# Branch A's channel pairs by seven block products, placed ahead of q, k, v, with z and gates behind

## The chip, the core and the metric

The kernel runs on one core of a Trainium2 chip. A core has TensorE (matrix products out of SBUF into the eight banks of PSUM), VectorE, ScalarE and GpSimd (elementwise work), SyncE, and DMA queues that SyncE, ScalarE and GpSimd issue to. The metric is device time in microseconds from the first to the last work of one execution; less is better.

## The reference

One decoder layer with two parallel branches, over a prompt of 1024 tokens and a sample of 8 sequences of 4 tokens (1056 tokens in all, 1024 channels, 8 heads of 128). All is float32.

```python
u = rmsnorm(x, norm_w)
a_b, a_c, a_h, a_z, qkv, b_z, b_beta, b_alpha, g_a, g_b = split(u @ w_in)
conv_out, new_a_buf = causal_conv(a_c * a_h, conv_a_buf, conv_a_w)      # width 3
y_a = (silu(a_z) * a_b * conv_out) @ w_out_a
q, k, v = silu(causal_conv(qkv, conv_qkv_buf, conv_b_w))                # width 4
o, S_new = gated_delta(l2norm(q) * 128**-0.5, l2norm(k), v, beta, g, S0)
y_b = (rmsnorm_head(o) * silu(b_z)) @ w_out_b
y = rmsnorm(x + (sigmoid(g_a) * y_a + sigmoid(g_b) * y_b) @ w_o, final_norm_w)
```

Within a chunk of tokens the gated delta rule needs the inverse of a unit lower triangular matrix and the products with decays; from chunk to chunk a state per head is carried on. The states of the convolutions and of the delta rule are outputs too.

## The kernel before

Tokens lie along the free axis, channels on the partitions. The normed input is kept in SBUF as two parts, uh (rounded) and ul (the rest), and every weight block of 128 output channels likewise as wh and wl; `mm` (L194) adds wh*uh, wl*uh and wh*ul over eight channel groups. A block is taken in three slices of 352 tokens (BLK, NBLK), 24 matmuls each, into one of four PSUM banks `pp`; other products use four banks `pd`. `load_w` fetches a block on SyncE's queue and splits it on ScalarE (L147) and VectorE (L149) while the block before it is in use; a list `seq` gives the order.

The order: x is loaded, normed, transposed (L270) and split; beta, alpha and the first k run in between; then the decay matrices `ee` of all heads are built from a DRAM scratch `gscr` (`gb`, L384 to L386); then for each head k, q and v (blocks, convolution, chunk products, results to DRAM scratch); then z (8 blocks, `act_proj`), branch A (for each of 8 channel groups the blocks c, h, z, b), the gates g_b and g_a (8 blocks each). Then follow w_out_a (8 blocks) on Y_A's factor, which `ya_` keeps in SBUF, w_out_b (8 blocks), and w_o (L928).

Behind the blocks from z on runs background work, written as generators: `invert` (the inverse, all on VectorE, L525 and L528, 62 steps), `merge` (of its halves, 18 steps, last product L567), `sample` (the delta rule of the sample, 27 steps), `scan` (the prompt's chunks, eight times two groups of four heads, 80 steps; loads `ld`, `tt`, `sz` on GpSimd's queue from L720). `pump` takes `rate` steps after each slice of a block; the rate is 1.1 up to the sample and 1.85 for the scan. Each generator's SBUF pool takes the place of the one before it, and `drain` runs the rest. During w_out_a the scan's result `oscr` is loaded and split for w_out_b (`o32`, one buffer, L883, L866, L867).

All of this is put into an order by a planner that simulates the engines and lets an instruction that is ready go ahead of others on its engine; `keep_in_program_order` pins one behind what was written before it on that engine.

Of the kernel before, what the change touches and what calls it, by code (L numbers as in the profile page):

```python
# [16 lines left out]
P = 128  # L17
D = 1024
# [7 lines left out]
NBLK = 3  # L26
NH = 8
# [20 lines left out]
def hybrid_step(ctx, tc, x_prompt, x_sample, state_conv_a, state_conv_qkv, state_delta, w_in, conv_a_w,  # L48
# [13 lines left out]
    pp = ctx.enter_context(tc.tile_pool(name="pp", bufs=4, space=PSUM))  # L62
    pd = ctx.enter_context(tc.tile_pool(name="pd", bufs=4, space=PSUM))
    dram = ctx.enter_context(tc.tile_pool(name="dram", bufs=1, space=DRAM))
    wp = ctx.enter_context(tc.tile_pool(name="wp", bufs=2))
    yp = ctx.enter_context(tc.tile_pool(name="yp", bufs=1))

    def ytile(k, shape=(P, TT)):
        return yp.tile(list(shape), F32, tag=f"ya{k}", name=f"ya{k}")

    def ptile(n=512):
        return pp.tile([P, n], F32, tag="pp", name="pp")

    def dtile(n=512):
        return pd.tile([P, n], F32, tag="pd", name="pd")
# [8 lines left out]
    oscr = dram.tile([NH, P, TT], F32, name="oscr")  # L84

# [1 line left out]
    ident = const.tile([P, P], F32, name="ident")  # L87
    make_identity(nc, ident)
    s_m, mid = opened(name="mid", bufs=1)
# [21 lines left out]
    newa = mid.tile([P, 18, 8], F32, name="newa")  # L111
    beta = mid.tile([P, 9, NH], F32, name="beta")
# [10 lines left out]
    s_m2, mid2 = opened(name="mid2", bufs=1, side="right")  # L123
    pastq = mid2.tile([P, 24, 24], F32, name="pastq")
    pasta = mid2.tile([P, 8, 16], F32, name="pasta")
    newq = mid2.tile([P, 27, 24], F32, name="newq")
    smp = mid2.tile([P, 3, NH, TS], F32, name="smp")
    szs = mid2.tile([P, NH, TS], F32, name="szs")
    gsb = mid2.tile([P, 2, 64, NT], F32, name="gsb")
    egs = mid2.tile([P, 64, NT], F32, name="egs")  # L130
    eps_ = mid2.tile([P, 6, 64], F32, name="epairs")

# [4 lines left out]
    s_u, up = opened(name="up", bufs=1)  # L137
# [4 lines left out]
    def load_w(w, col):  # L142
        n = 16 if w is w_in and col == C_BA else P
        wr = wp.tile([P, KC, n], F32, name="wr")
        nc.sync.dma_start(wr, w[:, col:col + n].rearrange("(k p) c -> p k c", p=P))
        wh = wp.tile([P, KC, n], F32R, name="wh")
        act.copy(wh, wr)  # L147
        wl = wp.tile([P, KC, n], F32R, name="wl")
        dve.tensor_tensor(wl, wr, wh.bitcast(F32), op=ALU.subtract)  # L149
        return wh, wl  # L150

    # every weight block is fetched and split while the one before it is in use
    seq = [(w_in, C_BA)]
    for h in range(NH):
        seq += [(w_in, C_K + h * P), (w_in, C_Q + h * P), (w_in, C_V + h * P)]
    seq += [(w_in, C_BZ + h * P) for h in range(NH)]
    for c in range(KC):
        seq += [(w_in, base + c * P) for base in (C_AC, C_AH, C_AZ, C_AB)]
    seq += [(w_in, base + c * P) for base in (C_GB, C_GA) for c in range(KC)]
    seq += [(w, c * P) for w in (w_out_a, w_out_b) for c in range(KC)]  # L160
    loaded = []
# [20 lines left out]
    def begin(w, col, mh, ml, ahead=True):  # L182
        assert seq[0][0] is w and seq[0][1] == col
        seq.pop(0)
        if not loaded:
            loaded.append(load_w(w, col))
        wh, wl = loaded.pop(0)
        if seq and ahead:
            loaded.append(load_w(*seq[0]))
# [31 lines left out]
    def conv_begin(ci):  # L221
# [3 lines left out]
        def evac(b, ps):  # L225
# [3 lines left out]
            if b == NBLK - 1:  # L229
                act.copy(sv[:, :, 3:7], ps[:, n:n + TS].rearrange("p (b t) -> p b t", t=NT))  # L230
# [741 lines left out]
```

## Time and profile before

| | us |
|---|---|
| median of 3 runs | 1473.81 |
| lowest, highest run | 1473.34, 1474.85 |
| profiled execution, span | 1474.3 |
| TensorE busy in it | 1430.8 (97%) |
| VectorE, ScalarE, GpSimd busy | 718.6, 459.9, 373.4 |

The profiled execution's own time is its span; it lies 0.5 us over the median of the runs. Matmuls are pipelined and a matmul's duration overlaps that of the next, so the distance between the starts of two matmuls is what one costs. The granted clock is given as a share of TensorE's full 2.4 GHz; the level below it is 1.2 GHz.

### The profile page before, as it was taken

The page shows a single profiled execution, that of the slowest core. Times are in us where ns is not written, and L with a number is a line of the kernel's source. Part 1 is how long each engine was busy: PE and PEld are TensorE (multiplying, and loading weights), DVE is VectorE, ACT ScalarE, POOL GpSimd, SP SyncE. Part 2 cuts the span into 40 slices and gives each one's busy share as a digit, 9 for nine tenths or more (in the row PEclk, how much of TensorE's full clock was granted, in tenths as well). Part 3 has the DMA queues.
Part 4 walks back from the last instruction along what each step waited for, and adds up shares of the span by engine and source line. Part 5 has one row for each costly group of instructions (what it writes and reads, how often), then busy time and mean ns, then how long its engine had stood idle before and what let it go on. Part 6 is the DMA issues. An engine that isn't in the chain of part 4 may idle for free.

```text
span 1474.3 us, 22239 instructions
## 1 busy us (share of the span) xinstructions
PE 1430.8 (97%) x9045; PEld 1373.8 (93%) x9045; DVE 718.6 (49%) x1262; ACT 459.9 (31%) x1120; POOL 373.4 (25%) x544
## 2 busy tenths in 40 slices
PE   8995899999999999999999999999999999999997
PEld 6995899999999999999999989999999999999785
DVE  6545454554548899994342543222222263355422
ACT  6436465555522111111110101333323331123111
POOL 2135543333240011113422244222221120001100
PEclk9997999999999999999999999999999999999999
DMA  5265675554383211115334166555765344343411
GB/s 171 63 100 101 157 199 130 131 141 114 97 229 104 73 43 44 44 44 143 95 91 131 32 179 208 180 180 182 244 224 183 117 148 131 100 145 111 152 43 47
DMA packets 135594, 186.18 MB, mean 126 GB/s; under 512 B 7735, under 2 KB 106177, under 8 KB 133444
## 3 DMA queue, kind: packets, MB, share of 16 engines
q0 software_dynamic: 26976, 108.10, 26.5%
q1 hardware_dynamic: 104480, 63.25, 14.7%
q10 hardware_dynamic: 4036, 13.41, 2.4%
q8 instruction: 71, 1.16, 0.3%
q14 instruction: 31, 0.25, 0.1%
HBM read 128.56 MB, written 56.18 MB: 125 GB/s over the span
## 4 chain that ended last, share of the span: by engine, by line
PE 85%; DMA 6%; issue 3%; POOL 2%; DVE 2%; ACT 1%; SPq 0%; DVEq 0%; POOLq 0%; ACTq 0%
PE pp L194 68%; PE pp L928 6%; DMA gb<-gscr 1%; PE pd L464 1%; DMA sb<-in_state_delta_dram 1%; PE pd L761 1%; PE pd L746 1%; PE pd L740 1%; DMA scr<-pk 1%; PE pd L729 1%; PE pd L760 1%; PE pd L622 1%; PE pd L683 1%; DMA qd<-gscr 1%; PE pd L567 1%
## 5 line engine op out<-in xcount | busy, mean ns | idle before, releaser
L194 PE MATMUL pp<-uh,wh 128*128 128x352 f32 (+1 forms) x1944 | 641.5, 330 | 0.0
L194 PE MATMUL pp<-uh,wl 128*128 128x352 f32 (+1 forms) x1944 | 632.1, 325 | 6.1 <-DVE wl L149 6.1
L194 PE MATMUL pp<-ul,wh 128*128 128x352 f32 (+1 forms) x1944 | 634.0, 326 | 0.0
L194 PEld LDWEIGHTS pp<-uh,wl 128*128 128x128 f32 (+1 forms) x1944 | 366.5, 189 | 11.1 <-DVE wl L149 6.7
L194 PEld LDWEIGHTS pp<-uh,wh 128*128 128x128 f32 (+1 forms) x1944 | 365.8, 188 | 5.6 <-issue 2.2
L194 PEld LDWEIGHTS pp<-ul,wh 128*128 128x128 f32 (+1 forms) x1944 | 365.5, 188 | 3.8 <-issue 2.0
L149 DVE TENSOR_TENSOR wl<-wr,wh 128x1024 fp32r<-128x1024 f32 (+1 forms) x97 | 130.7, 1347 | 183.5 <-ACT wh L147 183.2
L147 ACT CAST wh<-wr 128x1024 fp32r<-128x1024 f32 (+1 forms) x97 | 101.4, 1045 | 226.9 <-PE pp L194 225.7
L400 DVE SCALAR_TENSOR_TENSOR cv<-ext,vecT,cv 128x1080 f32<-128x1080 f32 x72 | 100.0, 1389 | 3.5 <-ACT cv L398 1.9
L701 ACT ACTIVATE zt<-pp 128x352 f32<-128x352 f32 x72 | 33.4, 465 | 180.9 <-PE pp L194 180.2
L525 DVE TENSOR_TENSOR pr<-xi,dl 128x1 f32<-128x1 f32 (+36 forms) x156 | 84.6, 542 | 5.1 <-POOL xi L511 0.8
L528 DVE TENSOR_REDUCE xi<-pr 128x1 f32<-128x1 f32 (+36 forms) x156 | 83.7, 537 | 4.8 <-DVE pr L525 0.2
L194 PE MATMUL pp<-yh,wh 128*128 128x352 f32 x192 | 62.2, 324 | 1.5 <-ACT yh L866 1.5
L194 PE MATMUL pp<-oh,wl 128*128 128x352 f32 x192 | 62.4, 325 | 0.0
L194 PE MATMUL pp<-yh,wl 128*128 128x352 f32 x192 | 62.2, 325 | 0.0
L194 PE MATMUL pp<-oh,wh 128*128 128x352 f32 x192 | 62.0, 323 | 0.0
L194 PE MATMUL pp<-ol,wh 128*128 128x352 f32 x192 | 61.8, 322 | 0.0
L194 PE MATMUL pp<-yl,wh 128*128 128x352 f32 x192 | 60.4, 325 | 1.4 <-POOL yl L867 1.3
L928 PE MATMUL pp<-woh,mh 128*128 128x512 f32 (+1 forms) x144 | 57.2, 397 | 1.1 <-ACT woh L911 1.1
L928 PE MATMUL pp<-wol,mh 128*128 128x512 f32 (+1 forms) x144 | 56.4, 395 | 0.0
L928 PE MATMUL pp<-woh,ml 128*128 128x512 f32 (+1 forms) x144 | 56.3, 391 | 0.0
L464 PE MATMUL pd<-kq 128*128 128x256 f32 x128 | 35.5, 403 | 16.6 <-ACT pk L442 16.6
(296 smaller groups left out, 1838.4 us busy)
## 6 DMA issues: line engine op xcount, KB each, us to landing
wr<-in_w_in_dram SPq DMA_DIRECT2D x80, 512.0 KB, 4.0
ld<-scr POOLq DMA_DIRECT2D x16, 1280.0 KB, 6.9
scr<-pk POOLq DMA_DIRECT2D x16, 768.0 KB, 4.4
sb<-in_state_delta_dram POOLq DMA_DIRECT2D x16, 512.0 KB, 4.9
zscr<-zt ACTq DMA_DIRECT2D x8, 528.0 KB, 2.6
gbscr<-zt ACTq DMA_DIRECT2D x8, 528.0 KB, 4.1
gascr<-zt ACTq DMA_DIRECT2D x8, 528.0 KB, 3.3
sg<-gascr POOLq DMA_DIRECT2D x8, 528.0 KB, 4.2
```

Of the source, the lines that this page charges most:

```text
L147: act.copy(wh, wr)
L149: dve.tensor_tensor(wl, wr, wh.bitcast(F32), op=ALU.subtract)
L194: pe.matmul(ps[:a.shape[2], :BLK], lhsT=a[:, k, :], rhs=m[k][:, sl], start=(k == 0 and i == 0), stop=(k == KC - 1 and i == 2))
L400: dve.scalar_tensor_tensor(cv, ext[:, j:j + LB], vecT[:, j * 24 + ci:j * 24 + ci + 1], cv, op0=ALU.mult, op1=ALU.add)
L464: pe.matmul(pt[:, i * 256:(i + 1) * 256], lhsT=kq[:, 0, c * P:(c + 1) * P], rhs=kq[:, :, c * P:(c + 1) * P], start=True, stop=True)
L525: ins = dve.tensor_tensor(pv, xi[q][:, 0:n, c0:j], bc(dl[j // Q4][:, j % Q4, c0:j], 1, [P, n, w]), op=ALU.mult)
L528: dve.tensor_reduce(xi[q][:, 0:n, j], pv, axis=AX.X, op=ALU.add, negate=True)
L567: pe.matmul(px[:64, h * H2:(h + 1) * H2], lhsT=t11[:, h, :], rhs=ww[:, h, :], start=True, stop=True)
L622: pe.matmul(pks[:, n * 8:(n + 1) * 8], lhsT=sb[:, b, :], rhs=kqn[:, :, n * NT:(n + 1) * NT], start=True, stop=True)
L683: pe.matmul(pt, lhsT=ktw[:, 0, g, :], rhs=we[:, hf * 4:(hf + 1) * 4, :].rearrange("p b v -> p (b v)"), start=True, stop=True)
L701: ins = act.activation(t[:, b * BLK:(b + 1) * BLK], ps[:, :BLK], func)
L928: pe.matmul(ps[:n, :], lhsT=a[k][:, sl], rhs=w[k][:, cs_], start=(k == 0 and i == 0), stop=(k == KC - 1 and i == 2))
```

## The change

Branch A goes in front of q, k, v. Its first channel group is done as before. For the other seven, the blocks c and h make a pair, and z and b another: 14 pairs. A pair is a 2 by 2 block product (two blocks of output channels, two halves of the tokens; the two halves of the input channels are summed over). It is done with seven products of four channel groups by 528 tokens, each in two slices of 264 (QT) and with the three matmuls of the split, in place of eight such products. The weight sums are made on VectorE ahead of each product (`prep`), the token sums once (`token_sums`, four calls, 12 VectorE instructions each); the seven results are combined in PSUM, by ScalarE copies (`kept`) and in the evictions. PSUM is laid out for it as three double banks `pb`, taken in turn, and two banks `pd`; x's transposes use both. After branch A the four and four banks of before are set up.

z, g_b and g_a follow q, k, v as 24 plain blocks. The background is one generator `chain` of the four parts at rate 2.0, and goes on through w_out_a. Y_A's factor goes to DRAM (`yscr`) and is loaded and split ahead of w_out_a; w_out_a's result goes to DRAM (`ascr`) too. After `drain` the scan's result is loaded through one buffer and split, and `ascr` is loaded, for w_out_b. The decay matrices are built two heads at a time between the heads. The norm's weight is broadcast by DMA and no longer by four matmuls.

```diff
+HT = TT // 2
+QT = HT // 2
...
     def ptile(n=512):
-        return pp.tile([P, n], F32, tag="pp", name="pp")
+        if "pb" in pools:
+            return btile()[:, 0, :n]
+        return pools["pp"].tile([P, n], F32, tag="pp", name="pp")
+    def btile():
+        i = nb[0] % 3
+        nb[0] += 1
+        return pools["pb"].tile([P, 2, 512], F32, tag=f"pb{i}", name=f"pb{i}")
...
+    PRODS = (1, 5, 6, 3, 7, 2, 4)
+    def prep(u):
...
+        if p == 5:
+            sums[pid] = sw.tile([P, 4, P], F32, tag="s", name="s1", bufs=2)
+            dve.tensor_tensor(sums[pid], a21, a22, op=ALU.add)
+        elif p == 6:
+            dve.tensor_tensor(sums[pid], sums[pid], a11, op=ALU.subtract)
+        elif p == 3:
+            dve.tensor_tensor(sums[pid], a12, sums[pid], op=ALU.subtract)
+        elif p == 7:
+            s3 = sw.tile([P, 4, P], F32, tag="s", name="s3", bufs=2)
+            dve.tensor_tensor(s3, a11, a21, op=ALU.subtract)
+        src = {1: a11, 2: a12, 4: a22, 7: s3 if p == 7 else None}.get(p, sums.get(pid))
+        w2 = wp.tile([P, 2, 4, P], F32R, tag="hl", name="w2", bufs=4)
+        act.copy(w2[:, 0], src)
+        dve.tensor_tensor(w2[:, 1], src, w2[:, 0].bitcast(F32), op=ALU.subtract)
+        return w2
...
+    def project_pair(c0, c1, evac):
...
+        def product(p, ps, start):
+            w2 = take()
+            th, tl = tok[p]
+            for g in range(2):
+                sl = slice(g * QT, (g + 1) * QT)
+                for k in range(4):
+                    for i, (a, m) in enumerate(((w2[:, 0], th), (w2[:, 1], th), (w2[:, 0], tl))):
+                        pe.matmul(ps[:, g, :QT], lhsT=a[:, k, :], rhs=m[:, k, sl], start=start and k == 0 and i == 0,
+                                  stop=(k == 3 and i == 2), skip_group_check=True)
+            return ps[:, :, :QT]
...
+        x, z = btile(), btile()
+        p1 = kept(product(1, x, True), "p1", 1)
+        p5 = kept(product(5, z, True), "p5", 2)
+        u2 = kept(product(6, x, False), "u2", 1)
+        evac(0, 1, product(3, z, False), u2)
+        evac(1, 1, product(7, x, False), p5)
+        evac(0, 0, product(2, btile(), True), p1)
+        evac(1, 0, product(4, x, False), None)
...
+    def token_sums(k):
...
+        r11, r12 = whole(tmp("p1", "r11"), 0, 0), whole(tmp("u2", "r12"), 0, HT)
+        r22, t3 = whole(tmp("p5", "r22", 2), 1, HT), tmp("s", "t3", 2)
+        dve.tensor_tensor(t3, r22, r12, op=ALU.subtract)
+        split(7, t3)
...
-        for i in range(2):
-            pt = ptile()
-            pe.matmul(pt, lhsT=ones[0:1, :], rhs=nwr[:, i * 512:(i + 1) * 512], start=True, stop=True)
-            dve.tensor_copy(nwb[:, i * 512:(i + 1) * 512], pt)
+    nc.scalar.dma_start(nwb, norm_w[0].partition_broadcast(P))
...
-            pt = dtile()
+            pt = dtile() if half else ptile()
...
+    token_sums(0)
+    for ci in range(KC):
+        branch_a(ci)
+        if ci == 1:
+            decays()
...
+        conv_chunk(8 + h, kq[:, 0])
         if h == 0:
-            conv_end(8, kq[:, 0], ext_k0, sv_k0)
+            decay_matrices(0)
+            decay_matrices(1)
+        elif h % 2 and h < NH - 1:
+            decay_matrices(h + 1)
+            decay_matrices(h + 2)
...
+    def chain():
+        for nm, fn, bufs in (("fp", invert, 1), ("fq", merge, 1), ("sp", sample, 1), ("cp", scan, 2)):
+            held, pl = opened(name=nm, bufs=bufs, side="right")
+            yield from fn(pl)
+            held.close()
+
+    background.append(chain())
+    rate[0] = 2.0
+    for h in range(NH):
+        act_proj(C_BZ + h * P, AF.Silu, zscr, h, szs[:, h, :])
     for h in range(KC):
-        act_proj(C_GB + h * P, AF.Sigmoid, gbscr, h, first=(h == 0))
+        act_proj(C_GB + h * P, AF.Sigmoid, gbscr, h)
     for h in range(KC):
         act_proj(C_GA + h * P, AF.Sigmoid, gascr, h, kouter=h == KC - 1)
...
+    for k in range(KC):
+        y32 = op_.tile([P, TT], F32, name="y32")
+        nc.sync.dma_start(y32, yscr[k])
+        pairs_.append(split(ha, y32, "y"))
...
+        nc.sync.dma_start(ascr[e], m)
+    drain()
...
+    for e in range(KC):
+        o32 = op_.tile([P, TT], F32, name="o32")
         aux.dma_start(o32, oscr[e])
         opair.append(split(hb, o32, "o"))
+    for e in range(KC):
+        ma.append(ytile(e))
+        nc.sync.dma_start(ma[e], ascr[e])
```

## Rows read from the trace of the kernel before

**Rows 1.** The page's first two parts: busy time per engine; granted clock in 40 slices.

```profile
PE 1430.8 (97%) x9045; PEld 1373.8 (93%) x9045; DVE 718.6 (49%) x1262; ACT 459.9 (31%) x1120; POOL 373.4 (25%) x544
...
PEclk9997999999999999999999999999999999999999
```

**Rows 2.** The page's chain that ended last, shares by engine.

```profile
PE 85%; DMA 6%; issue 3%; POOL 2%; DVE 2%; ACT 1%; SPq 0%; DVEq 0%; POOLq 0%; ACTq 0%
```

**Rows 3.** Busy time by stretch: length, engines with instructions, PEclk, DMA share, GB/s.

```profile
0.00:36.00 36.00, 28.98 (x162) 22.08 (x163) 24.55 (x40) 22.84 (x43) 9.12 (x26) 1.00 0.57 175
...
75.00:196.00 121.00, 98.04 (x570) 94.58 (x568) 57.71 (x70) 62.68 (x169) 61.79 (x74) 0.90 0.66 130
196.00:400.00 204.00, 204.00 (x1288) 200.86 (x1287) 102.89 (x153) 115.25 (x371) 70.91 (x133) 1.00 0.50 132
400.00:664.00 264.00, 264.00 (x1662) 263.59 (x1662) 215.50 (x376) 51.06 (x83) 42.14 (x64) 1.00 0.28 82
664.00:746.00 82.00, 82.00 (x696) 78.72 (x696) 31.66 (x41) 13.97 (x21) 31.90 (x45) 1.00 0.42 115
746.00:898.00 152.00, 149.91 (x895) 139.32 (x894) 71.03 (x190) 20.21 (x28) 51.31 (x49) 0.98 0.43 116
898.00:1182.00 284.00, 282.49 (x1968) 281.26 (x1966) 75.63 (x173) 96.50 (x283) 68.79 (x90) 1.00 0.57 191
1182.00:1273.00 91.00, 89.57 (x552) 88.84 (x552) 37.24 (x42) 18.57 (x19) 11.71 (x17) 1.00 0.41 124
```

**Rows 4.** Pieces of the chain of waits: start us, us, what.

```profile
415.91 276.07 PE pp L194 x1736
...
1379.98 86.94 PE pp L928 x372
```

**Rows 5.** Timeline of TensorE at three places: start us, us, instructions merged.

```profile
23.13 0.32 PE L194 MATMUL pp<-uh,wh 128*16 128x352 f32 x1
23.29 0.32 PE L194 MATMUL pp<-uh,wl 128*16 128x352 f32 x1
...
777.94 1.85 PE L622 MATMUL pd<-kqn,sb 128*128 128x8 f32 x16
...
1021.34 1.05 PE L740 MATMUL pd<-r,tt 128*128 128x128 f32 x8
```

**Rows 6.** Groups by line and shape: count, busy us, mean ns, idle before.

```profile
L149 DVE TENSOR_TENSOR wl<-wr,wh 128x1024 fp32r<-128x1024 f32 x96 | 130.4, 1358 | 183.5 <-ACT wh L147 183.2
...
L275 DVE TENSOR_TENSOR ul<-pd,uh 128x512 fp32r<-128x512 f32 x16 | 10.3, 681 | 1.0 <-ACT uh L274 1.0
...
L866 ACT CAST oh<-o 128x1056 fp32r<-128x1056 f32 x8 | 8.6, 1075 | 27.3 <-DMA o<-oscr 27.3
...
L867 DVE TENSOR_TENSOR ol<-o,oh 128x1056 fp32r<-128x1056 f32 x8 | 10.1, 1256 | 18.3 <-ACT oh L866 18.3
...
L525 DVE TENSOR_TENSOR pr<-xi,dl 128x1 f32<-128x1 f32 (+36 forms) x156 | 84.6, 542 | 5.1 <-POOL xi L511 0.8
L528 DVE TENSOR_REDUCE xi<-pr 128x1 f32<-128x1 f32 (+36 forms) x156 | 83.7, 537 | 4.8 <-DVE pr L525 0.2
```

**Rows 7.** Single lines: duration ns min/median/max, first and last start us.

```profile
L528 DVE TENSOR_REDUCE xi<-pr x156: 148/513/1204, 422.3 to 671.1; 128x1 f32<-128x1 f32 x4, 128x2 f32<-128x4 f32 x4, 128x3 f32<-128x9 f32 x4, 128x4 f32<-128x16 f32 x4
...
L567 PE MATMUL pd<-ww,t x128: 217/218/267, 697.6 to 745.5; 64*64 64x64 f32 x128
...
L701 ACT ACTIVATE zt<-pp x72: 455/464/480, 403.6 to 1174.9; 128x352 f32<-128x352 f32 x72
...
L720 POOL DMA_DIRECT2D ld<-scr x16: 534/536/597, 899.0 to 1123.2; - x16
```

**Rows 8.** DMA issues: count, KB each, median us from issue to landing.

```profile
ld<-scr POOLq DMA_DIRECT2D x16, 1280.0 KB, 6.9
...
gb<-gscr POOLq DMA_DIRECT2D x8, 512.0 KB, 8.9
...
o<-oscr POOLq DMA_DIRECT2D x8, 528.0 KB, 3.9
```

More of the change, by code (lines that the diff above doesn't have):

```diff
@@ L153, in hybrid_step @@
-    seq = [(w_in, C_BA)]
-    for h in range(NH):
[L155 to L161, printed above, removed]
+    tok = {}
+    PRODS = (1, 5, 6, 3, 7, 2, 4)
@@ new lines, in hybrid_step, with plan, plan_pair, w_cols @@
+    units, pairs, ready, raw, sums = [], [], {}, {}, {}
+    pos, nraw = [0], [0]
+    def plan(w, col):
+        units.append(("c", w, col))
+    def plan_pair(w, c0, c1):
+        pairs.append((w, c0, c1))
+        units.extend(("s", len(pairs) - 1, p) for p in PRODS)
+    def w_cols(w, col, n):
+        return w[:, col:col + n].rearrange("(k p) c -> p k c", p=P)
+    def fetch(pid, x):
+        if pid >= len(pairs):
+            return
+        i = nraw[0] % 3
+        nraw[0] += 1
+        t = pools["sw"].tile([P, KC, P], F32, tag="wx", name="wx") if i == 2 else wp.tile([P, KC, P], F32, tag="wr",
+                                                                                         name="wr")
+        nc.sync.dma_start(t, w_cols(pairs[pid][0], pairs[pid][1 + x], P))
+        raw[pid, x] = t
@@ new lines, in take @@
+    def take(ahead=True):
+        i = pos[0]
+        pos[0] += 1
+        if units[i][0] == "s":
+            at = PRODS.index(units[i][2])
+            if at in (0, 4):
+                fetch(units[i][1] + 1, at // 4)
+        room = 4
+        for j in range(i, min(i + 3 if ahead else i + 1, len(units))):
+            room -= 1 if units[j][0] == "s" else 0 if units[j][2] == C_BA else 2
+            if room < 0:
+                break
+            if j not in ready:
+                ready[j] = prep(units[j])
+        return ready.pop(i)
@@ new lines, in hybrid_step @@
+    plan(w_in, C_BA)
+    for base in (C_AC, C_AH, C_AZ, C_AB):
+        plan(w_in, base)
+    for c in range(1, KC):
+        plan_pair(w_in, C_AC + c * P, C_AH + c * P)
+        plan_pair(w_in, C_AZ + c * P, C_AB + c * P)
+    for h in range(NH):
+        for base in (C_K, C_Q, C_V):
+            plan(w_in, base + h * P)
+    for base in (C_BZ, C_GB, C_GA):
+        for h in range(NH):
+            plan(w_in, base + h * P)
+    for w in (w_out_a, w_out_b):
+        for c in range(KC):
+            plan(w, c * P)
@@ L182, in begin @@
     def begin(w, col, mh, ml, ahead=True):
[L183 to L189, printed above, removed]
+        u = units[pos[0]]
+        assert u[0] == "c" and u[1] is w and u[2] == col
+        wh, wl = take(ahead)
         def mm(ps, b, k):
@@ L707, in act_proj, with scan_step @@
         act.dma_start(dst[h], t)
-    background.append(invert())
-    rate[0] = 1.1
-    for h in range(NH):
-        act_proj(C_BZ + h * P, AF.Silu, zscr, h, szs[:, h, :])
     GH = 4
     state = [None, None]
-    def scan_step(c, g):
+    def scan_step(cp, c, g):
         hs = slice(g * GH, (g + 1) * GH)
@@ L780, in scan_step, with scan @@
         yield
-    def scan():
+    def scan(cp):
         for c in range(NCH):
-            gens = [scan_step(c, g) for g in range(2)]
+            gens = [scan_step(cp, c, g) for g in range(2)]
             while gens:
```

499 lines of the change are left out of this document (288 added, 211 removed).

## The prediction

> **What bounds the kernel now.** I read the page first. TensorE is busy for 97% of the span and its granted clock is full in all but a few slices [rows 1]; the chain that ended last is 85% TensorE [rows 2]. So whatever is to help must take work off TensorE, and whatever is to hurt must make TensorE wait. The table by stretches [rows 3] then shows where it waits today: 23 us out of 75 to 196 us (98.04 busy of 121, at a mean clock of 0.90), where the first heads wait for decay matrices, and hardly anywhere else. In the long stretch 400 to 1273 us the idle time is 2.1 + 1.5 + 1.4 = 5 us.
>
> Next the price of one matmul. 1736 of them, 352 columns wide, took 276.07 us: 159.0 ns each; 372 with 512 columns took 86.94 us: 233.7 ns [rows 4]. One block of 128 output channels is 72 matmuls, 11.45 us. Is that price the columns' or the weight load's? A 16-column stationary block has the same spacing, 23.13 to 23.29 us, so it is the columns. And 16 matmuls of 8 columns with full 128x128 weights fit into 1.85 us [rows 5], about 0.115 us each: that is the weight load's floor, and it lies under the column price of anything wider than 260.
>
> Last the background work (inverse, merge, sample, scan). It is one serial chain, today fed in behind 56 blocks and ended before the output projections. Its pieces [rows 7] tell how long it is when it isn't held back, which is what the change will ask.
>
> **Branch A's pairs.** Each of 14 pairs replaces 2 x 72 = 144 matmuls of 352 columns by 7 x 24 = 168 of 264. 264 columns were never run here. In proportion to 352 they take 159.0 x 264/352 = 119.3 ns; on the line through 352 and 512 columns 117.9; if the 12.3 ns that 352 columns take above 352/2.4 stay whole, 122.3. I take 119.3, since both widths measured are 8 to 10% above the columns at 2.4 GHz. A pair falls from 22.90 to 20.04 us, 14 pairs save **40.0 us** (33 to 43). VectorE must keep up: 7 subtractions and 4 sums over 512 columns at 0.68 [rows 6] are 7.5 us, five evictions over 528 columns some 3.5, so 11 of 20 us, 14 where the convolution's two passes fall in. That is hidden; uncovered it would be the saving and more.
>
> The Trainium skill, "TensorE: Matmul & The Clock Gate", section on the back-to-back issue gap, puts a warm matmul at N/2.4 plus about 2.5 ns. That would be 149.2 and 112.5 ns, and 36.2 us saved. The 352-column row disagrees, 159.0, so the measured price goes into the sum.
>
> **The first 90 us.** Before, matmuls of the first two blocks run between the transposes of x: in the first 36 us there are 162 matmuls [rows 3], of which 72 are transposes and 4 the norm's broadcast, so 86 are projection work, 13.7 us of it. After the change half of the transposes and the projections draw on the same three PSUM buffers in turn, so the first projection must wait until the seventh x block is evicted. I lose **8 us** (0 to 13.7). Then 48 VectorE passes for the token sums, 0.70 each, 33.6 us, plus 14 us of splits, evictions, convolution and first weight sums, stand against three blocks, 34.4 us of TensorE. The overhang is 14 us if nothing is done earlier; the planner moves ready work ahead, as the interleaved transposes show, so I take **5 us** (0 to 14). The norm weight's broadcast by DMA in place of four matmuls I set at nothing: x is fetched at the same time.
>
> **The start of q, k, v.** Today eight broadcasts of decays, 8.9 us each [rows 8], stand in front of the first heads, with VectorE and ScalarE queued behind them. Moved two at a time between heads, with the scratch written some 250 us earlier, they are out of the way; the per-head broadcast of the other decay stays and so does the first head's latency. **-22 us** (-10 to -32). The later heads run without gaps (204.00 of 204) and stay as they are.
>
> **The chain behind z and gates.** Here the change costs. Branch A's 32 blocks leave the stretch in which the chain ran. The first z eviction begins at 403.6 [rows 7], so z begins at 399.8; the last output projections begin at 1273. Between them lie 873.2 us: 64 blocks (732.8), 5 idle, so some 135 us of the chain's own TensorE work. After the change TensorE has 32 blocks there, 366.4, and the same 135: 501 us. Does the chain fit into 501?
>
> Step by step, from the beginning of z. The inverse starts at 422 [rows 7]: 22 us, of which most are its loads. Its 312 VectorE instructions take 84.6 + 83.7 = 168.3 us [rows 6], about 12 more between them, and a weight split of 1.36 falls in with every block, 17 of them, 23: 203 us. It can't be hastened by feeding it faster; at rate 2 it is VectorE that paces it, and the splits overtake it as they do now (in 400 to 664 VectorE is busy for 215.50 us and TensorE never waits). From its end, 671.6, to the merge's last matmul at 745.5 and copy, 746.6: 75 us of stores, loads and eight serial steps. The sample goes on to 898: 151 us, paced by sixteen loads of half a megabyte. The scan's first load is issued at 899.0 and takes 6.9 [rows 7, 8]: 10. One chunk of the scan, unhindered: the load of the next waits for the last product of this one, 6.9, then three groups of eight matmuls at 1.05 [rows 5], two rounds of VectorE and ScalarE of about 1, and the output product of sixteen matmuls, 1.8, with handovers 15; two groups share TensorE and DMA, so 17. Eight chunks: 136. The last output, its norm and store: 8. Sum 606. I take **580**, because the rows of merge and sample stood in a stream full of blocks, and the blocks run out at about 415 us, within the sample. Ends: 510 (merge and sample a fifth shorter, scan at 14 a chunk) and 650 (scan at 22). The chain is longer than the 501 us of TensorE work by 79, and TensorE waits for it.
>
> **The loads of branch B's output.** Today eight loads of 528 KB, each split before the next can use the buffer, are hidden behind w_out_a. One round is 3.9 to land [rows 8], 1.07 and 1.26 for the split [rows 6], 6.4 with handovers: 51 us. Now they stand behind the end of the chain, with nothing to cover them but the first product as far as PSUM holds it, some 13 us. **+38 us** (20 to 55; the loads of branch A's result run beside them). The reloads of Y_A's factor ahead of w_out_a cost nothing as long as the chain is what is late; without it they cost some 10.
>
> **Sum**, against the profiled span of 1474.3: in front of z, +366.4 (32 blocks) - 40.0 + 8 + 5 - 22 = +317.4. From z to the last projections, 580 + 38 - 873.2 = -255.2. Together +62.2, a span of 1536.5. The median of the runs lies 0.5 us under the profiled span, so **1536 us**.
>
> **The rivals.** *The chain fits behind the blocks* (faster). For it speaks that 187 steps at two a group end before the 192 that the blocks give out, so the order written down ends in time; against it that a step can't be run before its data are there. With TensorE as the bound, 501 us and 10 of reloads: 511 + 38 - 873.2 + 317.4 = -6.8, 1467 us; with the loads hidden too 1430. It decides from a chain under 518 us. *The emptied TensorE falls to its lower clock.* In 75 to 196 us, with 81% busy, the mean granted clock was 0.90; in a scan alone it is busy for about 60%. Every product of the scan then takes twice as long, some 5.5 us a chunk on its chain: +44, 1580 us. The Trainium skill, the same page's part on the clock gate's oscillation, says likewise that gaps between bursts bring the array back to half rate; the row agrees. *The narrower matmuls are not cheaper in time*: at 136.3 ns a piece, from weight loads (0.19 us each) or VectorE, the 40 us are gone: 1576 us. Against it stand rows 5.
>
> **Chances.** My forecast 0.58, with its own range 1500 to 1565 (chain 550 to 610); the chain that fits 0.16, of which 0.03 come out level; the lower clock 0.18; no cheaper matmuls 0.08. A difference of 0.2%, 3 us, is about what can be told from none. Faster 0.13, same 0.03, slower 0.84. The range takes in the lower clock and the edge of the chain that fits: 1465 to 1595.
>
> **What would show it.** Right: the 264-column matmuls 119 ns apart; z begins near 717; the inverse fills VectorE for some 200 us; TensorE has gaps from some 420 us after z's beginning until the last projections, with the scan alone on it; then eight split rounds of about 6.4 us with little TensorE work. Wrong: w_out_a's matmuls still running when the scan ends, then the chain was shorter than its rows; or TensorE waiting in branch A for weight sums.

## The result and the profile after

The changed kernel takes 1607.93 us (median of 4 runs, 1605.23 to 1609.61) against 1474.33 for the kernel before beside it: a ratio of 1.0905 [1.0883, 1.0926]. Slower, as forecast, but by 134 us instead of 62, and outside the range that ended at 1595. The profiled execution has a span of 1607.9 us, against 1474.3 before, and the sum of the prediction was 1536.5: **71.4 us are to be explained.**

The page first: busy time per engine, then TensorE's granted clock in 40 slices. They answer to [rows 1].

```profile
PE 1458.3 (91%) x9377; PEld 1381.1 (86%) x9377; DVE 837.6 (52%) x1464; ACT 520.3 (32%) x1224; POOL 373.9 (23%) x549
...
PEclk8999999999899999999999999899857777589999
```

TensorE fell from 97% of the span to 91%, and a dip has appeared between slices 30 and 36. The chain that ended last, 85% TensorE before [rows 2], follows only some 13% of the span here, so the stages are read from single lines instead: duration of one in ns (min/median/max), first and last start.

```profile
L304 PE MATMUL pb<-uh,w x672: 278/283/294, 93.0 to 377.6; 128*128 128x264 f32 x168
L955 ACT ACTIVATE zt<-pp x72: 447/464/577, 725.7 to 1002.8; 128x352 f32<-128x352 f32 x72
L785 DVE TENSOR_REDUCE xi<-pr x156: 143/506/1206, 752.2 to 984.0; 128x1 f32<-128x1 f32 x4, 128x2 f32<-128x4 f32 x4, 128x3 f32<-128x9 f32 x4, 128x4 f32<-128x16 f32 x4
L966 POOL DMA_DIRECT2D ld<-scr x16: 534/537/597, 1192.1 to 1335.3; - x16
L1099 POOL DMA_DIRECT2D o<-oscr x8: 528/528/556, 1363.3 to 1414.6; - x8
```

In order: the 2352 matmuls of the pairs fill 93.0 to 380.9, 121.9 ns apart. The first z eviction is at 725.7, so z begins at 721.9, where the sum has 399.8 + 317.4 = 717.2. The inverse starts at 752.2, 30 us after z, and ends at 984.3. The scan's first load is issued at 1192.1, its last store of output at 1362.6, and at 1363.3 the loads of branch B's output begin. From z's beginning to there are 641.4 us; the forecast for this chain was 580. Behind it come 244.6 us, where 201 + 38 = 239 were forecast. So 4.7 + 61.4 + 5.6 = 71.7, the 71.4 but for rounding: **by these marks nearly the whole error is the chain.** The mark for z's beginning turns out to be some 9 us off in the kernel before; the part on why the prediction was off says what that moves.

Where TensorE has nothing to do in it shows in the stretches from the inverse to the first product with `w_out_b` (the columns of [rows 3]):

```profile
752.00:985.00 233.00, 233.00 (x1467) 232.94 (x1466) 192.27 (x338) 48.54 (x82) 13.60 (x21) 1.00 0.37 107
985.00:1053.00 68.00, 64.09 (x556) 60.57 (x555) 24.38 (x29) 18.27 (x24) 25.02 (x37) 0.92 0.83 217
1053.00:1192.00 139.00, 119.05 (x633) 101.61 (x631) 60.27 (x184) 7.35 (x7) 43.52 (x42) 0.84 0.57 167
1192.00:1363.00 171.00, 115.34 (x672) 102.33 (x672) 47.50 (x146) 50.04 (x208) 59.67 (x83) 0.73 0.60 208
1363.00:1423.00 60.00, 29.79 (x95) 26.95 (x96) 10.34 (x9) 9.61 (x9) 5.13 (x10) 0.56 0.42 140
```

The third column is TensorE's. In the inverse it is full; in merge, sample, scan and the loads behind them it lacks 4 + 20 + 56 + 30 = 110 us, where before it lacked 5 in the whole of 664 to 1273 [rows 3]. What it waits for, over the whole span (total us, times, longest):

```profile
PE pp L266 <- ACT oh L1065: 32.9, 8, 9.6
PE pd L1020 <- ACT on L1016: 26.8, 16, 2.6
PE pd L986 <- DMA tt<-tscr: 17.6, 2, 15.2
...
PE pd L940 <- POOL we L934: 13.0, 5, 3.2
PE pd L605 <- DMA pq<-in_state_conv_qkv_dram: 12.3, 1, 12.3
```

The first four lines are the split of branch B's output, the scan and the sample. The last was not foreseen. The history of q, k, v moved with its stage to the end of branch A. Two of its three loads are issued at once, at 378.8 and 381.1. The third stands on ScalarE's queue behind exponentials of the decay matrices, which wait for their broadcasts; it is issued at 407.65, and TensorE waits 12.3 us for it.

And the inverse on VectorE, 752 to 985 (group, busy us, mean ns, idle just before it and what ended that):

```profile
L782 DVE TENSOR_TENSOR pr<-xi,dl 128x1 f32<-128x1 f32 (+36 forms) x156 | 84.7, 543 | 5.3 <-POOL xi L770 0.2
L785 DVE TENSOR_REDUCE xi<-pr 128x1 f32<-128x1 f32 (+36 forms) x156 | 83.8, 537 | 4.8
L185 DVE TENSOR_TENSOR wl<-wr,wh 128x1024 fp32r<-128x1024 f32 x20 | 24.5, 1226 | 21.8 <-ACT wh L183 21.8
L751 DVE COPY so<-pd 120x128 f32<-120x128 f32 (+2 forms) x6 | 1.7, 285 | 8.3 <-DMA out_dram<-so 8.3
```

The inverse's own work is what the prediction took from [rows 6], 168.5 us. But the third line shows VectorE idle for 21.8 us in front of the weight splits: the split stands at the head of VectorE's queue, waits for ScalarE's rounding, which waits for a buffer of weights, and the inverse's next step, ready to run, stands behind it. The fourth line stands for stores of states through one small buffer. They were there before; now branch A's state is stored with them, and VectorE waits 8.3 us for the buffer within the inverse's stretch. In the kernel before, over its inverse (422 to 672), these two waits are 16.9 and 3.3 us:

```profile
L149 DVE TENSOR_TENSOR wl<-wr,wh 128x1024 fp32r<-128x1024 f32 x22 | 32.4, 1475 | 16.9 <-ACT wh L147 16.9
L492 DVE COPY so<-pd 120x128 f32<-120x128 f32 (+1 forms) x4 | 1.1, 283 | 3.3 <-DMA out_dram<-so 3.3
```

### The profile page after: what moved, and what is told of

Same layout as the page of the kernel before. It is cut to its first block, busy times and chain, and to the rows that moved or that the text cites. A ratio compares the mean times of both kernels' runs of the same rounds, so it can differ in the third digit from the quotient of the medians.

```text
span 1607.9 us, 23413 instructions
## 1 busy us (share of the span) xinstructions
PE 1458.3 (91%) x9377; PEld 1381.1 (86%) x9377; DVE 837.6 (52%) x1464; ACT 520.3 (32%) x1224; POOL 373.9 (23%) x549
## 5 line engine op out<-in xcount | busy, mean ns | idle before, releaser
L266 PE MATMUL pp<-uh,wh 128*128 128x352 f32 x1152 | 374.8, 325 | 0.0
L266 PE MATMUL pp<-ul,wh 128*128 128x352 f32 x1152 | 373.9, 325 | 0.0
L266 PE MATMUL pp<-uh,wl 128*128 128x352 f32 x1152 | 370.6, 322 | 0.0
L266 PEld LDWEIGHTS pp<-uh,wh 128*128 128x128 f32 x1152 | 216.7, 188 | 2.2 <-ACT ext L644 1.5
L266 PEld LDWEIGHTS pp<-uh,wl 128*128 128x128 f32 x1152 | 217.1, 188 | 0.4
L266 PEld LDWEIGHTS pp<-ul,wh 128*128 128x128 f32 x1152 | 216.8, 188 | 0.5
L304 PE MATMUL pb<-uh,w 128*128 128x264 f32 x672 | 124.0, 284 | 0.0
L304 PEld LDWEIGHTS pb<-uh,w 128*128 128x128 f32 x672 | 103.9, 188 | 0.0
L658 DVE SCALAR_TENSOR_TENSOR cv<-ext,vecT,cv 128x1080 f32<-128x1080 f32 x72 | 96.8, 1344 | 12.3 <-ACT cv L656 10.6
L304 PE MATMUL pb<-ul,w 128*128 128x264 f32 x336 | 95.2, 283 | 0.0
L782 DVE TENSOR_TENSOR pr<-xi,dl 128x1 f32<-128x1 f32 (+36 forms) x156 | 84.7, 543 | 5.3 <-POOL xi L770 0.2
L785 DVE TENSOR_REDUCE xi<-pr 128x1 f32<-128x1 f32 (+36 forms) x156 | 83.8, 537 | 4.8
L304 PEld LDWEIGHTS pb<-ul,w 128*128 128x128 f32 x336 | 63.3, 188 | 0.0
```

Of the source, the lines that this page charges most:

```text
L266: pe.matmul(ps[:a.shape[2], :BLK], lhsT=a[:, k, :], rhs=m[k][:, sl], start=(k == 0 and i == 0), stop=(k == KC - 1 and i == 2))
L304: pe.matmul(ps[:, g, :QT], lhsT=a[:, k, :], rhs=m[:, k, sl], start=start and k == 0 and i == 0, stop=(k == 3 and i == 2), skip_group_check ...
L658: dve.scalar_tensor_tensor(cv, ext[:, j:j + LB], vecT[:, j * 24 + ci:j * 24 + ci + 1], cv, op0=ALU.mult, op1=ALU.add)
L782: ins = dve.tensor_tensor(pv, xi[q][:, 0:n, c0:j], bc(dl[j // Q4][:, j % Q4, c0:j], 1, [P, n, w]), op=ALU.mult)
L785: dve.tensor_reduce(xi[q][:, 0:n, j], pv, axis=AX.X, op=ALU.add, negate=True)
```

## The experiments

Each is an edit of the changed kernel unless it says otherwise. The changed kernel's stages (z begins 721.9, inverse 752.2 to 984.3, scan 1192.1 to 1363.3) are the comparison.

**1. The pairs taken out, the order kept.**

```diff
-        plan_pair(w_in, C_AC + c * P, C_AH + c * P)
-        plan_pair(w_in, C_AZ + c * P, C_AB + c * P)
+        for base in (C_AC, C_AH, C_AZ, C_AB):
+            plan(w_in, base + c * P)
...
```

> The changed order kept, the 14 pairs done as plain blocks, no token sums. The chain theory (the time from the beginning of z to the last step of the scan is set by the serial chain, everything in front by TensorE): the front grows by 14 x (144 x 159.0 - 168 x 121.9 ns) = 34 us less the token sums' 0 to 5 us, so about 1608 + 31 = 1639 us (1632 to 1645), the chain unchanged at some 641 us. Rival, the pairs themselves cost the time (VectorE sums, narrower matmuls): 1608 us or less.

1630.96 us (1629.72 to 1635.15), ratio 1.105 [1.102, 1.108]. The first z eviction comes at 745.4, 19.7 later, and the chain behind it is the same, 643.9. The stretch of the pairs itself is 32.7 longer; 12.3 of the difference is given back at the wait for `pq`, which only the faster branch A runs into. So the pairs are a real gain, worth some 23 us in the end, and the rest of the change, the order above all, is the loss: 1631 - 1477 = 154 us against the kernel before that ran beside it.

**2. More cover.** Eight more blocks (the g_b blocks once more, results read by nobody), 92 us of TensorE work, among the chain. If the chain is what is late, they cost nothing.

```diff
-    for base in (C_BZ, C_GB, C_GA):
+    for base in (C_BZ, C_GB, C_GA, C_GB):
...
```

> Eight more plain blocks (the gate g_b a second time, its result left in a scratch that nothing reads) behind z and gates: 8 x 11.45 = 92 us more TensorE work. The chain theory: they fall into time in which TensorE waits for the chain, so 1608 us, give or take 15 (the chain's matmuls stand among more blocks, the clock of the scan stays higher for longer). Rival, the amount of work on TensorE sets the end: 1700 us.

1648.74 (1647.5 to 1650.0), ratio 1.1165 [1.1138, 1.1193]: +41, neither 0 nor 92. From z to the end of the scan 679.6 instead of 641.4: merge and sample 223 us instead of 208, the scan 194 instead of 171. So the chain is late, but it has no length of its own: blocks that stand between its steps lengthen it. The blocks bring loads of weights and work for ScalarE and VectorE too; this run alone does not show that it is TensorE's queue.

**3. The order written down.** Chain steps issued twice as densely.

```diff
-    rate[0] = 2.0
+    rate[0] = 4.0
```

> The background's rate 4 in place of 2, so that all 187 steps are written down within half the blocks. The chain theory: the steps wait for their data and not for their place in the order, so 1608 us, give or take 10. Rival, the order written down holds the chain back: the part of it that is paced by slices shortens, 1550 to 1590 us.

1613.82 (1610.4 to 1616.7), ratio 1.0921 [1.0884, 1.0958]. The order in which the program gives out the steps isn't what holds the chain.

**4. A shorter inverse.** The last ten of its 63 columns are left out, so this kernel computes only part of the inverse.

```diff
-        for j in range(1, H2):
+        for j in range(1, 54):
```

> The last ten of the inverse's 63 columns are left out (j from 1 to 53, so that the inverse is incomplete): 80 VectorE instructions, 57.5 us, which with the splits and waits among them took from 908.5 to 984.5 us in the changed kernel, 76 us. The chain theory: everything behind comes that much earlier, except that merge and sample then stand among more blocks, which the run with more cover showed to cost something: 1608 - 76 = 1532 us, at most 15 more. Rival, TensorE or the loads behind the chain set the end: 1590 us or more.

1565.36 (1559.1 to 1567.0), ratio 1.0584 [1.0551, 1.0617]. The inverse takes 156.3 us instead of 232.1, 75.8 less; the time falls by 43 (by 50 in the profiled execution). Merge 78 instead of 68, sample 144 instead of 140, scan 180 instead of 171: with the inverse over earlier, more blocks are left to stand among the later steps. The expected 1532 was the simple subtraction, and it fails.

**5. The weight splits of z and the gates on GpSimd**, so that the inverse has VectorE to itself; first all of them (a), then only those of the last four z blocks, of g_b and of the first three g_a blocks (b).

```diff
-            dve.tensor_tensor(wl, wr, wh.bitcast(F32), op=ALU.subtract)
+            late = w is w_in and (C_BZ <= col < C_BA or col >= C_GA)
+            (pool if late else dve).tensor_tensor(wl, wr, wh.bitcast(F32), op=ALU.subtract)
```

In (b) the condition is:

```diff
+            late = w is w_in and (C_BZ + 4 * P <= col < C_BA or C_GB <= col or C_GA <= col < C_GA + 3 * P)
```

> The low parts of the weights of z and the gates are subtracted on GpSimd in place of VectorE. The chain theory: the inverse, 232 us on VectorE, loses 20 splits (24.5 us) and the 21.8 us in which VectorE waits at a split for ScalarE's rounding, and everything behind it comes as much earlier: 1608 - 46 = 1562 us, less if GpSimd and VectorE hinder each other (1562 to 1590). Rival, the inverse is hidden and only the scan and the loads behind it count: 1608 us; if a GpSimd split of 2 to 3 us were late for TensorE: more than 1608.

(a) 1637.76 (1635.8 to 1641.8), ratio 1.1094 [1.1063, 1.1126]: a miss, 30 us slower. The inverse did get shorter, 791.7 to 1000.4, 208.7 us; but it starts 39 us later (6 of them are z's own later beginning). The same GpSimd queue issues the stores of the states, now between splits of 2.4 us and more, and VectorE, which copies the states through the one small buffer ahead of the inverse, waits 45.8 us for them.

> As the run with the splits on GpSimd, but only from the fifth z block on (the last three blocks before the inverse's end stay on VectorE too), so that GpSimd's queue is free when the inverse's copies and loads are issued; all else as in the changed kernel (1607.9). Theory (the 22 us that VectorE waits for ScalarE at the head of its queue, and the splits' own 24 us, stand in the inverse's chain, and only the late start ate the gain): the inverse starts at 752 to 760 us and takes 208 to 215 us instead of 232: 1585 to 1595. Rival (what the chain gains in the inverse it gives back behind it, or GpSimd is late again): 1605 to 1640.

(b) 1610.45 (1606.91 to 1610.99), ratio 1.0899 [1.0879, 1.0919]: no gain. The inverse starts at 756.3 and takes 217.5 us, 15 less; merge and what follows give it back (merge's end 76 us behind the inverse instead of 68, sample 144 instead of 140). Under both edits the inverse's own multiplies became slower. VectorE's groups in the inverse of (a), 791 to 1001:

```profile
L783 DVE TENSOR_TENSOR pr<-xi,dl 128x1 f32<-128x1 f32 (+36 forms) x156 | 114.0, 731 | 5.5
L786 DVE TENSOR_REDUCE xi<-pr 128x1 f32<-128x1 f32 (+36 forms) x156 | 84.0, 538 | 5.4
```

The reductions take what they took, the multiplies 114.0 us instead of 84.7. The timeline of (a) at one of GpSimd's splits (start, duration, engine) shows how:

```profile
849.05 0.49 DVE L783 TENSOR_TENSOR pr<-xi,dl 128x320 f32<-128x320 f32 x1
849.14 2.66 POOL L186 TENSOR_TENSOR wl<-wr,wh 128x1024 fp32r<-128x1024 f32 x1 [8.78 <-ACT wh L183]
...
849.58 0.49 DVE L786 TENSOR_REDUCE xi<-pr 128x16 f32<-128x320 f32 x1
850.10 1.74 DVE L783 TENSOR_TENSOR pr<-xi,dl 128x16 f32<-128x16 f32 x1
```

A multiply of 16 columns takes 1.74 us and ends at 851.84, as GpSimd's split ends at 851.80. Of the 28 multiplies that overlap a split, 18 are longer, by 29.3 us in sum; 17 of them start after the split, one 0.16 us before it. The other ten, like the first line here, had all started before the split and have kept their length, and so have the 128 that overlap none.

**6. Two buffers for branch B's output.**

```diff
-        o32 = op_.tile([P, TT], F32, name="o32")
+        o32 = op_.tile([P, TT], F32, name="o32", bufs=2)
```

> Two buffers in place of one for the loads of the scan's result. The loads theory (eight rounds of load, rounding and subtraction one after another stand on the path): the load of the next runs beside the split of this one, a round falls from 6.4 to about 4 us, 8 x 2.4 = 19 us less: 1589 us (1584 to 1598). Rival, the reloads of w_out_a's result beside them take the bandwidth, or TensorE is late anyway: 1605 us.

1592.69 (1590.8 to 1595.7), ratio 1.0783 [1.0748, 1.0818]. The eight issues of these loads, in this run:

```profile
L1099 POOL DMA_DIRECT2D o<-oscr x8: 528/528/558, 1369.8 to 1396.9; - x8
```

27 us from first to last instead of 51, and from the first load to the end 219 us instead of 244.6. 15 come off the time, as the stages in front come 6 us later in this run. The uncovered loads are where the prediction put them, and the one buffer is half of it.

**7. Three of branch A's groups back** behind z and g_b, as 12 plain blocks.

```diff
-    for c in range(1, KC):
+    for c in range(1, 5):
         plan_pair(w_in, C_AC + c * P, C_AH + c * P)
         plan_pair(w_in, C_AZ + c * P, C_AB + c * P)
...
+        if base is None:
+            for c in range(5, KC):
+                for b_ in (C_AC, C_AH, C_AZ, C_AB):
+                    plan(w_in, b_ + c * P)
```

> Three of branch A's channel groups (12 plain blocks) go back behind z and the gate g_b, the other five stay in front, four of them in pairs. The chain theory: z begins 6 x 20.5 = 123 us earlier, the chain behind it grows with the blocks that now stand among it as the run with more cover showed, 38 us for 92, so 57 for 137: 1608 - 123 + 57 = 1542 us (1520 to 1560). Rival, the work on TensorE sets the end, or the pairs' saving does: 3 x (45.8 - 41) = 14 us more, 1622 us.

1543.01 (1539.3 to 1547.1), ratio 1.0441 [1.0409, 1.0473]: 65 us back. The chain starts 122 us earlier and is 696 us long, 55 more: 12 blocks, 137 us, lengthen it by 0.4 of their own time, as the eight of experiment 2 did (38 of 92). The blocks that the change took away are what the chain lacks as cover.

**8. The clock in the scan.** The rival of the emptied TensorE said 1580, and the granted clock of the scan is 0.73. The first try to raise it used extra matmuls whose place is fixed:

```diff
+    def filler():
+        fl = ptile()
+        for i in range(3):
+            tc.keep_in_program_order(pe.matmul(fl[:, :P], lhsT=ident, rhs=ident, start=True, stop=True))
...
```

> Three more 128x128 matmuls, whose products nobody reads, at each of five phases of every scan chunk (15 a chunk, 8 chunks and two groups, some 14 us in all at the higher clock), so that TensorE is busier in the scan; all else as in the changed kernel (1607.9). In that kernel the scan takes 171 us at a granted clock of 0.73 and its groups of eight matmuls 1.9 to 2.05 us. Theory (the lower clock stretches the scan by some 17 us): the granted clock there rises to 0.9 or more, the groups fall towards 1.05 us and the scan to 150 to 160 us: 1590 to 1600. Rival (the scan is paced by its loads and by VectorE and ScalarE, the clock counts little): the scan stays at 168 to 185 us and the time at 1605 to 1622.

1722.8 (1721.76 to 1725.89), ratio 1.1668 [1.1644, 1.1693]: far off both, and no answer on the clock, since fixing their place drew the blocks with it. The products with `w_out_a`, 1014 to 1152 in the changed kernel, now run from 1298 to 1480. Merge, sample and scan of this run:

```profile
979.00:1036.00 57.00, 37.18 (x320) 34.33 (x320) 10.57 (x16) 4.63 (x8) 24.75 (x36) 0.50 0.46 104
1036.00:1158.00 122.00, 67.48 (x187) 42.49 (x186) 41.18 (x156) 0.00 (x0) 39.59 (x36) 0.53 0.38 101
1158.00:1476.00 318.00, 292.47 (x2099) 287.42 (x2100) 83.47 (x189) 79.75 (x246) 64.85 (x91) 0.96 0.55 183
```

It tells something else: alone, at a granted clock of 0.50 and 0.53, merge and sample take 57 + 122 = 179 us; with blocks between their steps, at 0.92 and 0.84, 68 + 139 = 207. Company costs them more than the clock does. It need not be TensorE's queue: the DMA share fell as well, from 0.83 and 0.57 to 0.46 and 0.38, and the two are not separated here.

The second try lets the extra matmuls use the scan's operands and PSUM buffers, so that the blocks keep their places; three (a) or six (b) for each phase.

```diff
+    def filler(t):
+        fl = dtile()
+        for i in range(3):
+            pe.matmul(fl[:, :P], lhsT=ident, rhs=t, start=True, stop=True)
...
```

> The same question as the run of the pinned extra matmuls, which moved the projection blocks into the scan and so told nothing of the clock. Here the three 128x128 matmuls of each phase (products read by nobody) work on the phase's own operand and write to the scan's own PSUM buffers, so the blocks keep their places in TensorE's queue; some 53 us of extra work in the scan at 0.22 us a piece. Changed kernel 1607.9, its scan 1192 to 1363 us at a granted clock of 0.73. Theory (the clock stretches the scan by some 17 to 35 us): granted clock above 0.9, groups of eight matmuls at 1.05 us instead of 1.9 to 2.05, the scan 150 to 162 us: 1587 to 1600. Rival (the scan is paced by its loads, VectorE and ScalarE, so the clock gives nothing and the extra matmuls delay): 1608 to 1650.

> As the run with three, with six extra matmuls a phase, some 106 us of extra TensorE work within the scan, so that the clock is full whatever the gaps. Theory (clock): groups of eight at 1.05 us; the scan no longer than with three by more than the work that does not fit in its gaps: 150 to 175 us, 1587 to 1612. Rival: the scan grows by the extra work, 1640 to 1700.

(a) 1638.15 (1636.9 to 1640.14), ratio 1.1094 [1.1076, 1.1113]; (b) 1661.48 (1659.54 to 1669.08), ratio 1.1259 [1.1232, 1.1286]. The scan of each, first (a):

```profile
1195.00:1389.00 194.00, 153.25 (x1140) 142.75 (x1140) 47.44 (x146) 50.36 (x208) 59.30 (x82) 0.90 0.52 181
```

and (b):

```profile
1200.00:1415.00 215.00, 191.70 (x1608) 185.33 (x1608) 46.78 (x146) 50.25 (x208) 58.79 (x82) 0.96 0.48 164
```

The clock rises from 0.73 to 0.90 and 0.96, and the scan does not shorten: 171, 195, 216. The first three add 24 us, the second three 21. The extra matmuls stand in the chain's way themselves, so these runs do not price the clock; the next one's trace does, in part.

**9. The scan's own buffers.** What paces a chunk at 20.5 us is seen in the changed kernel's timeline of one chunk (start, duration; what ended the idle time before):

```profile
1238.88 1.13 DVE L979 SCALAR_TENSOR_TENSOR r<-pd,ngam,ld 128x128 f32<-128x128 f32 x4 [3.00 <-PE pd L975]
1240.93 2.05 PE L975 MATMUL pd<-S,ld 128*128 128x128 f32 x8 [1.45 <-DMA ld<-scr]
...
1242.77 1.91 PE L986 MATMUL pd<-r,tt 128*128 128x128 f32 x8
...
1244.72 1.12 DVE L979 SCALAR_TENSOR_TENSOR r<-pd,ngam,ld 128x128 f32<-128x128 f32 x4 [2.27 <-PE pd L986]
1245.13 0.63 PE L986 MATMUL pd<-r,tt 128*128 128x128 f32 x2 [0.44 <-DVE r L979]
```

The second group's product is out at 1242.98, but its `r` is computed from 1244.72 on, when the first group's product (line 986) has read the one buffer of `r`. The edit gives `r`, `on` and `ot` two.

```diff
...
-        ot = cp.tile([P, GH, P], F32, name="ot", bufs=1)
+        ot = cp.tile([P, GH, P], F32, name="ot", bufs=2)
```

> In the changed kernel (1607.9, scan 1192 to 1363, 20.9 us a chunk) three small tiles of the scan, r, on and ot, have one buffer for both groups; the second group's r is written only when the first group's product has read it, and TensorE's queue holds both groups in one order. Here each has two; all else as it was. Theory (the two groups hold each other up through these tiles, which is why the extra matmuls for the clock gave nothing): a chunk falls to the 17 to 19 us of the prediction's count, the scan to 140 to 160 us: 1577 to 1597. Rival (the chunk's own chain of product, copy and load paces it): scan 167 to 173 us: 1604 to 1610.

1599.29 (1595.75 to 1602.12), ratio 1.0819 [1.0782, 1.0856]. The scan's loads, in this run:

```profile
L966 POOL DMA_DIRECT2D ld<-scr x16: 534/534/598, 1204.5 to 1331.0; - x16
```

18.1 us a chunk (126.5/7) instead of 20.5 (143.2/7), the scan 152 us instead of 171, at about the forecast's 154. Of these 19 us 9 arrive: in this run z begins 3 us later than in the changed kernel, and merge and sample take 9 longer. Which of the three tiles counts was not tried one by one.

The clock has a part in the scan too, and this trace shows it. The first group's loads are issued at 1259.32, 1275.59 and 1293.80; the two chunks between them hold the same instructions:

```profile
1259.30:1275.60 16.30, 12.28 (x91) 11.17 (x90) 6.15 (x20) 6.31 (x28) 7.32 (x11) 0.90 0.73 258
1275.60:1293.80 18.20, 13.59 (x91) 12.48 (x90) 6.15 (x20) 6.28 (x28) 7.29 (x11) 0.81 0.67 231
1268.75 1.13 PE L975 MATMUL pd<-S,ld 128*128 128x128 f32 x8 [0.62 <-DVE r L979]
1269.72 1.95 PE L986 MATMUL pd<-r,tt 128*128 128x128 f32 x16
1284.93 2.05 PE L975 MATMUL pd<-S,ld 128*128 128x128 f32 x8 [1.21 <-DVE ot L1022]
1286.77 3.11 PE L986 MATMUL pd<-r,tt 128*128 128x128 f32 x16
```

At a granted clock of 0.90 the second group's product and the two behind it take 2.9 us from start to end, at 0.81 5.0, and the chunk is 1.9 us longer. The next chunks repeat it: 16.5 us at 0.90, 18.1 at 0.81. In the changed kernel, at 0.75, these products are as slow (2.05 and 1.91 above) and a chunk takes 20.2 to 20.5. So, as an estimate from these chunks, the buffers bring some 2 us a chunk beside equally slow products, and the clock up to 2 more.

**10. The pieces together**: the edits of 6, 5 (b) and 9 in one kernel.

> The changed kernel with the pieces together that cost its chain: two buffers for the loads of branch B's output (alone 15 us), late splits on GpSimd (alone nothing), two buffers for the scan's r, on and ot. If the pieces add up: 1589 less what the scan's tiles give, and 5 to 15 for the inverse now that the scan is shorter: 1555 to 1585. Rival (as with the shortened inverse, what one step gains the next gives back): 1585 to 1595. Under neither does it come near the kernel before, 1474: the order of the change is what costs, not one of its buffers.

1565.86 (1565.33 to 1571.23), ratio 1.0606 [1.0563, 1.065]. 42 us come off, twice the 21 that the three brought alone (15, -3 and 9): scan 155 us, the inverse 217.5, the loads 27. It is still 89 us behind the kernel before.

**11. What the change holds that the old order can use**: the kernel before, with only its decay matrices made two at a time between the heads.

```diff
+    def decay_matrices(h):
+        gb = ee[h]
...
+            if h % 2 and h < NH - 1:
+                decay_matrices(h + 1)
+                decay_matrices(h + 2)
```

> The kernel before, with one part of the change alone: the decay matrices built two at a time between the heads of q, k, v. The theory on the start of q, k, v: of the 23 us in which TensorE waited between 75 and 196 us, and of the time at the lower clock there, about 22 us go: 1474 - 22 = 1452 us (1444 to 1464). Rival, it is the first head's own latency that TensorE waits for: 1470 us or more.

1454.96 (1451.6 to 1459.3), ratio 0.9846 [0.9819, 0.9873]: **1.5% less than the kernel before, and less than the changed one.** The stretch of [rows 3] in which TensorE had 98.04 us of work in 121, in this run:

```profile
75.00:196.00 121.00, 114.91 (x714) 113.13 (x713) 77.51 (x93) 78.12 (x215) 74.47 (x93) 0.97 0.66 166
```

17 of its 23 idle us are filled, at a clock of 0.97 instead of 0.90, and the first z eviction comes at 380.5 instead of 403.6. The 22 us that the prediction gave this part are there.

## Why the prediction was off

**Right.** The direction and its mechanism: a serial chain loses its cover, TensorE waits for it, the loads of branch B's output stand bare behind it, and experiment 6 shows their price. Their rounds were sized well but for the first two: 8.1 and 10.3 us, then 6.4 to 6.7 where 6.4 was taken. The eight take 57.6 us (1363.3 to 1420.9) instead of 51, and that is the 5.6 us by which the end is late.

**Luck: the front of z.** +317.4 was forecast, and between the two marks, 399.8 and 721.9, lie 322. But the mark in the kernel before was misread. It is the first eviction of z less one slice, and ScalarE comes late to that eviction there, with two slices of z done. TensorE's first matmul of z in the kernel before, the eviction, and the first matmul in the changed kernel:

```profile
390.34 0.41 PE L194 MATMUL pp<-uh,wh 128*128 128x352 f32 x1
403.64 0.82 ACT L701 ACTIVATE zt<-pp 128x352 f32<-128x352 f32 x2 [0.69 <-PE pd L464]
721.38 0.41 PE L266 MATMUL pp<-uh,wh 128*128 128x352 f32 x1
```

TensorE comes to z 331 us later, 14 more than forecast. 6 of these are the 264 columns, 121.9 ns where 119.3 were taken. Some 12 us instead of 8 were lost among the transposes of x (82 matmuls in the first 36 us instead of 162). 12.3 were lost at `pq`, which nothing in the sum stands for: the queue that the moved history loads came to stand in was not looked through. Against that, the 5 taken for the token sums were not needed (TensorE is busy for all of 36 to 93 us), and the decays earned 23 instead of 22 (experiment 11). Together that is some 16, near the 14. The misread mark hid 9 of the 14 and put them into the chain.

**Wrong: the step "The chain behind z and gates", 580 us; it measured 641.4.** (Its terms add up to 605, not 606.) Term by term, from z's beginning as it was marked:

- start of the inverse, 22 taken, 30 measured. It did not get longer: from TensorE's first matmul of z it is 32.0 us before (390.3 to 422.3) and 30.8 here (721.4 to 752.2). The 22 come from the late mark.
- the inverse, 203 taken, 232 measured. Its instructions were counted rightly, 168.3 and 23 for splits, and so were the gaps between its steps (10.1, where 12 were taken). What was left out is waits on VectorE's queue: 21.8 us for ScalarE's rounding, and 10 for the stores of states (line 751, 1.7 and 8.3). The row was in the trace of before: the group of line 149 in [rows 6] carries 183.5 us of idle time over the span, nearly all ended by ScalarE, 16.9 of it within the inverse, and the inverse itself spans 422.3 to 671.1, 249 us, in [rows 7] (with some of branch A's work on VectorE among it). "The splits overtake it as they do now" is true of TensorE alone.
- merge and sample, 226 taken before the cut, 208 measured: 18 of the 26 us that the forecast cut off as a whole.
- the scan with its first load and last store, 154 taken before the cut, 171 measured; the rest of the cut, 8, had no ground. Experiment 9 gives 152 once the two groups no longer share the buffers of `r`, `on` and `ot`: the handovers were counted, the wait of one group for the other was not. The lower clock is in the 17 as well, and the runs do not divide them.

8 + 29 + 8 + 17 = 62, the error between the marks. Counted from TensorE's first matmul of z, the 71.7 are 14 in front, 52 in the chain and 5.6 behind it.

**The rivals.** The chain that fits did not come: no run brought it under 518. The lower clock came, 0.73 in the scan, and 1580 lies nearer to the measurement than 1536, but for another reason. The whole scan is 17 us over its term, not 44, and a part of that is the shared buffers. What the clock takes there stays open; an estimate from experiment 9 is up to 2 us a chunk, some 15 in all. The narrow matmuls are cheaper, as the sum had them.

**What the prediction's form missed.** It treated the chain as a length to compare with the blocks' 501 us. Experiments 2, 4 and 5 show that the two lengthen each other: 92 us of added blocks cost 41, 76 us taken from the inverse bring 43 to 50, 15 taken from it later bring nothing. In the scan extra matmuls alone do it (experiment 8), so there it is TensorE's queue; for merge and sample the DMA queues are not ruled out. Why the late splits bring nothing alone, and the three edits of experiment 10 together twice their sum, was not settled. Between runs whose edits lie elsewhere, z's beginning moved by up to 6 us, and merge and sample took 207 to 217.

## What to carry to other kernels

Before moving work ahead of a serial chain, add up what is left to cover the chain, and set the length that each stage shows in the trace (here 249 us for the inverse) beside the sum of its instructions (203): the difference is waits, and other work on the same queue, and 29 of these 46 us stayed (232). Read where a stage begins from the engine that the sum is about, not from one that runs behind it. Look through each queue that a moved load or store comes to stand in. And a change of order often carries a small independent gain, here the decay matrices between the heads, that the old order can have for itself.

## What was not expected of the hardware

A VectorE multiply with two inputs in SBUF that starts while GpSimd runs a subtraction of two SBUF inputs stands still until GpSimd is done: 16 columns took 1.74 us and ended within 0.04 us of GpSimd's split, the 18 that were longer cost 29.3 us, and reductions beside the same splits lost nothing (84.0 us against 83.8). The Trainium skill, "SBUF — State Buffer", section "Summary: rules for kernel authors", says that when VectorE has two SBUF inputs while GpSimd reads SBUF, the second to issue blocks until the first is done; the trace agrees, and of the eleven multiplies that had started before a split ten lost nothing. So the splits on GpSimd were not off the inverse's path: of the 46 us (24.5 + 21.8) that left VectorE's queue, 29 came back as slower multiplies.

The clock counts on a chain of short steps even where TensorE is idle a third of the time: in experiment 9 the same eight matmuls took 1.13 or 2.05 us, and the chunk 16.3 us at a granted clock of 0.90 and 18.2 at 0.81. Yet merge and sample were fastest at 0.50 and 0.53, alone, 179 us instead of 207: what stood beside them, in TensorE's queue or on the DMA queues, counted more there than how fast TensorE ran.
